# Sums of FFN weights made by accumulating DMAs in place of VectorE and GpSimd operations

## The chip, the cores and the metric

The kernel runs on one core of a Trainium2 chip (trn2). The metric is the device time of one execution in microseconds (us). Of the kernel before there are three timed runs and one profiled execution. Engine names are those of the profile: PE (TensorE), DVE (VectorE), ACT (ScalarE), POOL (GpSimd) and SP (the engine that only issues DMAs). PEld is PE's loading of weights.

## What is computed

One step of a two-layer streaming encoder for 1024 prompt frames and 64 frames of a running stream, 1088 columns in all, model width 1024, in fp32. Layer 0 is an SSD mixer (a gated state-space scan), layer 1 a chunk-band attention. Each is followed by a SwiGLU feed-forward layer (FFN) with a hidden width of 2816; the change touches only this part and what is done ahead of it:

```python
def swiglu(u, w_in, w_out):
    g, up = jnp.split(u @ w_in, 2, axis=-1)
    return (jax.nn.silu(g) * up) @ w_out
...
        xp = xp + rmsnorm(swiglu(rmsnorm(xp, nw[2]), ffn_w_in[layer], ffn_w_out[layer]), nw[3])
        xs = xs + rmsnorm(swiglu(rmsnorm(xs, nw[2]), ffn_w_in[layer], ffn_w_out[layer]), nw[3])
```

## The kernel before

**Products.** Every fp32 operand is split into a high part, rounded to the fp32r type that PE reads, and a low part, the rest. A product is three matmuls: high by high, high by low, low by high (L1338, L1339, L1340 in the FFN's first half). The high part of a weight tile is a cast on ACT, the low part a subtraction (method part, L354 and L355), on DVE unless another engine is named; or ACT writes the negated high part and an accumulating DMA from POOL adds the weights from DRAM to it (L350).

**Stages.** The head (weights, norms) lasts to about 97 us, the SSD scan with the input projection to 655, the output projection to 906, FFN-1 (u @ w_in, silu, product) of layer 0 from 918 to 1331, FFN-2 (@ w_out) to about 1575, the attention to about 2113 with its projection behind it, FFN-1 of layer 1 from 2260 to 2672 and FFN-2 to the end at 2918.

**FFN-1.** There are 22 pairs of weight tiles, gate and up. The columns are two halves, b = 0 with 512 and b = 1 with 576, each made of two quarters. A pair with its two quarters and two halves of the inner dimension is a 2 by 2 block product, which run_pair makes with seven products instead of eight (PRODS, in Strassen's manner). Six of the pairs are first run plainly for b = 0 (plain_pairs); then 16 pairs run for both halves, the first of them all seven products of b = 0 and then those of b = 1 ("apart"), the others alternately; at the end the six pairs of the start run for b = 1 alone. In this text the first pair, the middle and the tail of FFN-1 are these three parts. A product is 12 matmuls, of 256 columns for b = 0 and 288 for b = 1.

**Weights of a pair** (method pair). SP loads two raw tiles of 512 KB: r0 holds the blocks b11 and b21, r1 holds b12 and b22. POOL makes two differences into ta and tb (L302: b22 - b12, L303: b12 - b11), DVE completes them with two sums (L320, L321). Then r0, ta and tb are each split (L354, L355 on DVE), and b22 is split with its low half on POOL (L355, engine POOL; for two pairs per layer by the accumulating DMA L350). Rings of buffers: raw (2, and lent ones called rx), hl for split tiles (3), half for b22 (2), tt for ta and tb (2).

**Evacuation.** The seven products leave PSUM by adds on DVE (L1353, L1355, L1359, L1362, L1363, L1365, L1370) and activations on ACT (L1356, L1366). Two products per pair are made on POOL: u (L1367) and c (L1371). put_hid stores them to DRAM, and sum_one (L1469) and sum_two (L1477) make on DVE the sums of hidden tiles that FFN-2's seven products need; these wait for u and c.

**Weight sums for FFN-2.** FFN-2 is also a seven-product block, and four of its seven weight operands are sums of blocks of w_out. They are made during FFN-1: load_sums loads blocks (SP), sum_weights makes four DVE operations per job (L1414; 40 jobs, called from hook behind certain products), and SP stores the result to a DRAM tensor wsum, from which FFN-2 loads its tiles.

**What sets the order.** The order on PE is written by hand (the Stream st, with a planner clock st.t that advances by the cost of the matmuls). The other engines take their instructions in an order that a scheduler makes ahead of time, by priorities and its own estimates; each engine and each DMA queue then works strictly in that order. W.behind, W.loaded and the function behind fix places by dependences that cost no wait at run time.

**The scan.** It handles groups of output tiles of the input projection; in each group DVE evacuates the matmuls (L762), multiplies the decay matrices MT that SP has loaded (L886 the load, L895 the operation), POOL makes xe (L918), from which PE makes sp (L926), and y products (L963) that SP stores (yscr, L964).

## Time and profile before

| what | us |
|---|---|
| median of the timed runs | 2917.82 |
| lowest and highest of three | 2912.8, 2917.83 |
| profiled execution | 2919.82 |
| its span | 2918.0 |
| PE busy in it | 2852.8 |
| DVE, ACT, POOL busy | 2191.3, 1383.5, 726.5 |

Times inside the profile count from the start of its span. A row of a timeline gives the start, the duration, the engine, the line of the kernel, the operation, its output and inputs by name and shape, and in brackets how long the engine had been idle before it and which instruction's end released it. The granted clock is PE's, 1.00 at full speed. Busy times of matmuls overlap, so PE's rate is better read from the number of matmuls in a stretch.

### The profile page before, as it was taken

Reading aid. Unit: us, or ns where it says so; the run is one execution under the profiler, and the core shown is the slowest. Engines: PE = TensorE matmul, PEld = TensorE weight load, DVE = VectorE, ACT = ScalarE, POOL = GpSimd, SP = SyncE. Lnnn points to the kernel's source line nnn. Section 1 sums busy time; section 2 is a strip of 40 time slices with the busy share of each in tenths; the row PEclk is TensorE's granted clock in tenths of the full one; section 3 lists DMA queues with packets and bytes.
Section 4 is the critical chain, followed back from the end, with each engine's and each line's share of the span. In section 5 each row is a group of like instructions: output and inputs, shape, how many; then the busy total and the mean of one; then the engine's idle time right before and its main releaser. Section 6 shows DMA issues by size and latency. Waiting matters only on the chain. (4 is left out here: it accounts for less than half of the span.)

```text
span 2918.0 us, 58367 instructions
## 1 busy us (share of the span) xinstructions
PE 2852.8 (98%) x22094; PEld 2805.7 (96%) x22094; DVE 2191.3 (75%) x4994; ACT 1383.5 (47%) x2564; POOL 726.5 (25%) x900
## 2 busy tenths in 40 slices
PE   8999999999999999999998999999999999999999
PEld 8999999999999999999997899999999999999998
DVE  7987888885768667785569778777778876776567
ACT  6654546454444222244445556556565322334443
POOL 1333333331122343441021000000041334343011
PEclk9999999999999999999999999999999999999999
DMA  4423333244565556446564222222377455555656
GB/s 139 126 99 101 107 101 103 96 125 144 177 183 157 168 175 194 160 159 209 183 194 156 61 80 79 74 64 82 96 220 214 152 180 175 178 176 169 203 189 196
DMA packets 271530, 426.23 MB, mean 146 GB/s; under 512 B 25360, under 2 KB 202736, under 8 KB 271248
## 3 DMA queue, kind: packets, MB, share of 16 engines
q1 hardware_dynamic: 268016, 411.94, 44.4%
q0 software_dynamic: 3232, 10.56, 2.0%
q8 instruction: 174, 2.85, 0.4%
q14 instruction: 108, 0.88, 0.1%
HBM read 313.74 MB, written 104.19 MB: 143 GB/s over the span
## 5 line engine op out<-in xcount | busy, mean ns | idle before, releaser
L480 PE MATMUL mm<-r,hl 128*128 128x384 f32 (+2 forms) x1704 | 569.0, 334 | 6.1 <-DVE vt L1872 3.9
L481 PE MATMUL mm<-r,hl 128*128 128x384 f32 (+2 forms) x1704 | 551.4, 324 | 2.4 <-DVE r L1586 2.4
L482 PE MATMUL mm<-r,hl 128*128 128x384 f32 (+2 forms) x1704 | 551.1, 323 | 2.1 <-DMA hl<-in_w_in_dram 1.4
L1339 PE MATMUL px<-r,hl 128*128 128x288 f32 (+1 forms) x1184 | 348.1, 294 | 0.0
L480 PEld LDWEIGHTS mm<-r,hl 128*128 128x128 f32 x1704 | 323.4, 190 | 8.4 <-DVE vt L1872 4.2
L481 PEld LDWEIGHTS mm<-r,hl 128*128 128x128 f32 x1704 | 323.2, 190 | 3.3 <-DVE r L1586 3.0
L482 PEld LDWEIGHTS mm<-r,hl 128*128 128x128 f32 x1704 | 322.0, 189 | 2.8 <-DMA hl<-in_w_in_dram 1.7
L1340 PE MATMUL px<-r,hl 128*128 128x288 f32 x1056 | 312.7, 296 | 3.2 <-DVE hl L355 3.1
L1338 PE MATMUL px<-r,hl 128*128 128x288 f32 x1056 | 311.3, 295 | 2.8 <-DVE u L1353 2.1
L355 DVE TENSOR_TENSOR hl<-raw,hl 128x1024 fp32r<-128x1024 f32 (+2 forms) x172 | 193.7, 1127 | 99.1 <-ACT hl L354 98.8
L1712 PE MATMUL po<-r,hl 128*128 128x288 f32 (+1 forms) x856 | 246.9, 288 | 0.1
L1710 PE MATMUL po<-r,hl 128*128 128x288 f32 (+1 forms) x856 | 246.9, 288 | 0.0
L1711 PE MATMUL po<-r,hl 128*128 128x288 f32 (+1 forms) x856 | 246.9, 288 | 0.0
L1339 PEld LDWEIGHTS px<-r,hl 128*128 128x128 f32 x1184 | 223.0, 188 | 0.0
L354 ACT CAST hl<-raw 128x1024 fp32r<-128x1024 f32 (+2 forms) x172 | 166.5, 968 | 114.0 <-PE po L1712 34.3
L1340 PE MATMUL px<-rx,hl 128*128 128x256 f32 x768 | 215.0, 280 | 3.7 <-DVE hl L355 3.6
L1338 PE MATMUL px<-rx,hl 128*128 128x256 f32 x768 | 214.5, 279 | 1.5 <-ACT hl L354 1.5
L1340 PEld LDWEIGHTS px<-r,hl 128*128 128x128 f32 x1056 | 199.4, 189 | 4.6 <-DVE hl L355 4.6
L1338 PEld LDWEIGHTS px<-r,hl 128*128 128x128 f32 x1056 | 199.5, 189 | 3.7 <-DVE u L1353 2.5
L1339 PE MATMUL px<-rx,hl 128*128 128x256 f32 x640 | 178.9, 280 | 0.0
L1710 PEld LDWEIGHTS po<-r,hl 128*128 128x128 f32 x856 | 161.5, 189 | 0.0
L1712 PEld LDWEIGHTS po<-r,hl 128*128 128x128 f32 x856 | 160.9, 188 | 0.3 <-DVE hl L355 0.3
(385 smaller groups left out, 8152.2 us busy)
## 6 DMA issues: line engine op xcount, KB each, us to landing
raw<-in_w_f_dram SPq DMA_DIRECT2D x104, 512.0 KB, 4.2
raw<-in_w_in_dram SPq DMA_DIRECT2D x40, 512.0 KB, 3.9
MT<-ascr SPq DMA_DIRECT2D x48, 384.0 KB, 4.4
r<-hscr SPq DMA_DIRECT2D x58, 288.0 KB, 4.2
raw<-in_w_so_dram SPq DMA_DIRECT2D x32, 512.0 KB, 3.8
r<-in_w_f_dram SPq DMA_DIRECT2D x48, 288.0 KB, 3.4
wsum<-r SPq DMA_DIRECT2D x24, 576.0 KB, 3.4
r<-hscr SPq DMA_DIRECT2D x40, 256.0 KB, 4.2
```

The source lines that it names most:

```text
L354: self.nc.scalar.copy(h, v)
L355: (eng or self.eng or self.nc.vector).tensor_tensor(lo, v, h, op=ALU.subtract)
L480: PE.matmul(ps[:, :n], h_, xh, start=(first and i == 0), stop=False)
L481: PE.matmul(ps[:, :n], h_, xl, start=False, stop=False)
L482: PE.matmul(ps[:, :n], l_, xh, start=False, stop=(last and i == nk - 1))
L1338: PE.matmul(ps, wh, ah[:, k, :], start=(k == 0), stop=False)
L1339: PE.matmul(ps, wh, al[:, k, :], start=False, stop=False)
L1340: PE.matmul(ps, wl, ah[:, k, :], start=False, stop=(k == 3))
L1710: PE.matmul(ps, wh, xh, start=(k0 > 0 and i == ks[0]), stop=False)
L1711: PE.matmul(ps, wh, xl, start=False, stop=False)
L1712: PE.matmul(ps, wl, xh, start=False, stop=(k0 == 0 and i == ks[-1]))
```

## The change

The signs of the seven-product scheme are turned, so that the sums of weight blocks are plain sums without a difference. In the place of tb and ta stand T (s1), with the halves b11 + b12 and b12 + b22, and S (s2), with the halves b11 + b12 + b22 and the sum of all four. They are made as follows.

- **Pairs of FFN-1.** SP loads two 512-wide blocks into T (L282). When the planner's clock is 5.0 us further (ACC_W), POOL issues an accumulating DMA of 512 KB into T (L288). DVE makes S from T and r0 in two sums (L330, L331). S (s2) and T (s1) are split as before. The second raw load is only b22, 256 KB. The low half of b22 is always made by ACT's negated copy (L358) and an accumulating DMA (L359). The POOL operations L302, L303 and L355 are gone.
- **Sums for FFN-2.** weight_sums makes wsum of both layers during the scan, in DRAM: for each of four blocks per layer, copies by SP (L608 with 1.44 MB, L610 twice with 0.72 MB) and accumulating DMAs by POOL (L609 with 1.44 MB, L611 and L612 with 0.72 MB). Three steps are issued in each group of the scan from the fifth on. load_sums, sum_weights and their buffers are gone.
- **Products.** P4 now comes before P5, and some evacuations subtract where they added; their number is the same, and PE's order is the same.

DVE has 4120 rows of instructions instead of 4240, ACT 2100 instead of 2045, POOL 822 instead of 839, SP 1211 instead of 1248. The core of the diff:

```diff
+ACC_W = 5.0
...
+            while self.tq and self.tt.free():
+                it = self.tq.pop(0)
+                it["T"] = self.tt.get()
+                self.loaded = self.nc.sync.dma_start(it["T"].rearrange("p (e k) -> p e k", e=2), it["two"][0])
...
+                self.aq.append((self.clock() + ACC_W, it))
+            while self.aq and self.aq[0][0] <= self.clock():
+                it = self.aq.pop(0)[1]
+                self.nc.gpsimd.dma_start(it["T"], it["two"][1], accum_op=ALU.add)
+                it["added"] = True
...
-            ta, tb = it["T"] = self.tt.get(), self.tt.get()
-            g = self.nc.gpsimd.tensor_tensor
-            g(ta[:, 512:], b22, b12, op=ALU.subtract)
-            g(tb[:, :512], b12, b11, op=ALU.subtract)
...
-            self.part(it, "b22", self.half, b22, self.nc.gpsimd, it["pacc"] and it["src"][1][:, 512:])
...
+            self.part(it, "b22", self.half, r1[:, :512], None, it["src"][1])
...
+            T, S = it["T"], self.t2.get()
...
-                v(ta[:, :512], ta[:, 512:], b11, op=ALU.add)
-                v(tb[:, 512:], b21, ta[:, :512], op=ALU.subtract)
+                v(S[:, :512], T[:, 512:], r0[:, :512], op=ALU.add)
+                v(S[:, 512:], S[:, :512], r0[:, 512:], op=ALU.add)
...
-        for key, src in (("ta", ta), ("tb", tb)):
+        for key, src, ring in (("s2", it["S"], self.t2), ("s1", it["T"], self.tt)):
...
-    (P1, "r0", 0, 0), (P6, "ta", 0, 1), (P2, "r0", 512, 2), (P7, "ta", 512, 5),
-    (P5, "tb", 0, 3), (P4, "tb", 512, 6), (P3, "b22", 0, 4),
+    (P1, "r0", 0, 0), (P6, "s2", 0, 1), (P2, "r0", 512, 2), (P7, "s1", 512, 5),
+    (P4, "s2", 512, 6), (P5, "s1", 0, 3), (P3, "b22", 0, 4),
...
+    def weight_sums(layer):
+
+        w2, z, n = w_f2[layer], wsm_[layer], HF * P
...
+        steps = []
+        for g in range(4):
+            a, b, to = w2[2 * g], w2[2 * g + 1], z[:, g]
+            steps.append((
+                lambda g=g, to=to: sp(nc.sync.dma_start(to[:, 2:4, :], w2[2 * g:2 * g + 2, :, :n].rearrange("e p k -> p e k"))),
+                lambda b=b, to=to: pool(G.dma_start(to[:, 2:4, :], b.rearrange("p (e k) -> p e k", e=2), accum_op=ALU.add, max_dma_last_dim=4 * n)),
+                lambda a=a, to=to: (sp(nc.sync.dma_start(to[:, 0, :], to[:, 3, :])), sp(nc.sync.dma_start(to[:, 1, :], a[:, n:]))),
+                lambda a=a, to=to: pool(G.dma_start(to[:, 0, :], a[:, :n], accum_op=ALU.add)),
+                lambda to=to: pool(G.dma_start(to[:, 1, :], to[:, 0, :], accum_op=ALU.add)),
+            ))
+        for f in range(5 + 3):
+            for g in range(4):
+                if 0 <= f - g < 5:
+                    yield steps[g][f - g]
...
-        for grp in order:
+        staged = chain_of(weight_sums(0), weight_sums(1))
+        for i, grp in enumerate(order):
+            for _ in range(3 if i > 3 else 0):
+                next(staged, lambda: None)()
...
-                if (p_, t_ % 2) in ((P2, 0), (P7, 0), (P7, 1)):
-                    w = next((w for w in workers[::-1 if (p_, t_ % 2) == (P7, 0) else 1] if "job" in w), None)
-                    if w:
-                        sum_weights(w, last)
```

Three places show what moves. The first is POOL in the tail of layer 0's FFN-1, two pairs and a part of a third, before (u and c are the hidden products, half and tt weight tiles):

```order
L1367 TENSOR_TENSOR u_15602<-u_15602,c_15624 128x288
L355 TENSOR_TENSOR half<-raw,half 128x512
L303 TENSOR_TENSOR tt<-raw,rx 128x512
L1371 TENSOR_TENSOR c_15624<-p_15551,u_15566 128x288
L302 TENSOR_TENSOR tt<-raw 128x512
L1367 TENSOR_TENSOR u_15739<-u_15739,c_15761 128x288
L355 TENSOR_TENSOR half<-raw,half 128x512
L303 TENSOR_TENSOR tt<-raw,rx 128x512
L1371 TENSOR_TENSOR c_15761<-p_15685,u_15700 128x288
```

The same two pairs on POOL now:

```order
L1407 TENSOR_TENSOR u_15510<-u_15510,c_15525 128x288
L359 DMA half<-in_w_f_dram 128x512
L1411 TENSOR_TENSOR c_15525<-p_15458,u_15473 128x288
L288 DMA tt<-in_w_f_dram 128x1024
L1407 TENSOR_TENSOR u_15648<-u_15648,c_15663 128x288
L359 DMA half<-in_w_f_dram 128x512
L1411 TENSOR_TENSOR c_15663<-p_15593,u_15608 128x288
```

Between u and c stood two tensor operations on weights, and now there is one DMA issue; the sum for T is issued behind c.

The second place is DVE ahead of the first pair of layer 0's FFN-1, before (raw and tt are weight tiles, hl<-raw is the low half of r0, r<-r is work on the activations):

```order
L320 TENSOR_TENSOR tt<-tt,raw 128x512
L1312 TENSOR_TENSOR x<-mmx,x 128x256
L321 TENSOR_TENSOR tt<-raw,tt 128x512
L355 TENSOR_TENSOR hl<-raw,hl 128x1024
L1197 TENSOR_TENSOR r<-r 128x1152 x4
L355 TENSOR_TENSOR hl<-tt,hl 128x1024
```

And now (t_11192 is S; L364 is the former L355, L1236 the former L1197):

```order
L330 TENSOR_TENSOR t_11192<-tt,raw 128x512
L1352 TENSOR_TENSOR x<-mmx,x 128x256
L331 TENSOR_TENSOR t_11192<-t_11192,raw 128x512
L1236 TENSOR_TENSOR r<-r 128x1152 x4
L364 TENSOR_TENSOR hl<-raw,hl 128x1024
L1236 TENSOR_TENSOR r<-r 128x1152
L364 TENSOR_TENSOR hl<-t_11192,hl 128x1024
```

The low half of r0 has moved from ahead of the four r<-r operations to behind them, and stands behind the sums that wait for T.

The third place is SP's queue in the scan, before, around the fifth group (raw are weights of the input projection, yscr stores y, MT and ea are loads of decay factors):

```order
L262 DMA raw<-in_w_in_dram 128x1024 x2
L964 DMA yscr<-y 128x384 x2
L262 DMA raw<-in_w_in_dram 128x1024
L964 DMA yscr<-y 128x320
L262 DMA raw<-in_w_in_dram 128x1024
L886 DMA MT<-ascr 128x2x384 x2
```

And now at the same place:

```order
L268 DMA raw<-in_w_in_dram 128x1024 x2
L608 DMA wsum_116<-in_w_f_dram 128x2x1408 x2
L1000 DMA yscr<-y 128x384 x2
L268 DMA raw<-in_w_in_dram 128x1024
L1000 DMA yscr<-y 128x320
L268 DMA raw<-in_w_in_dram 128x1024
L610 DMA wsum_116<-wsum_116 128x1408
L610 DMA wsum_116<-in_w_f_dram 128x1408
L608 DMA wsum_116<-in_w_f_dram 128x2x1408
L1000 DMA yscr<-y 128x384
L922 DMA MT<-ascr 128x2x384
```

Five copies for the weight sums have come between the loads and stores, three of them between the last weight load and the next MT.

More of the change, by code (lines that the diff above doesn't have):

```diff
@@ L1 @@
 from contextlib import ExitStack
+from itertools import chain as chain_of
 import concourse.bass as bass
@@ L234, with __init__ @@
 class Weights:
-    def __init__(self, nc, raw, hl, half, tt):
-        self.nc, self.raw, self.hl, self.half, self.tt = nc, raw, hl, half, tt
+    def __init__(self, nc, raw, hl, half, tt, t2):
+        self.nc, self.raw, self.hl, self.half, self.tt, self.t2 = nc, raw, hl, half, tt, t2
         self.tc, self.pri, self.nsc = None, 0, 0
@@ L255, in plan @@
             self.sq.append(it)
+            if "two" in it:
+                self.tq.append(it)
     def load(self):
@@ L272, in advance @@
             moved = False
+            while self.tq and self.tt.free():
+                it = self.tq.pop(0)
+                it["T"] = self.tt.get()
+                self.loaded = self.nc.sync.dma_start(it["T"].rearrange("p (e k) -> p e k", e=2), it["two"][0])
+                if self.behind is not None:
+                    self.tc.add_manual_dep(self.loaded.ins, self.behind.ins.name, ORDER, reason="place in the order")
+                self.aq.append((self.clock() + ACC_W, it))
[3 more added lines that the diff above has]
+                it["added"] = True
             while self.lq and any(r.free() for r in self.raws):
@@ L316, in pair @@
             return False
-        if "sums" not in it:
+        if "b22" not in it and self.half.free():
+            self.part(it, "b22", self.half, r1[:, :512], None, it["src"][1])
+            it["of"][1].put()
+            return True
+        if "S" not in it:
+            if "added" not in it or not self.t2.free():
+                return False
+            T, S = it["T"], self.t2.get()
+            it["S"] = S
             v = self.nc.vector.tensor_tensor
             with self.tc.high_priority(self.pri):
-                v(ta[:, :512], ta[:, 512:], b11, op=ALU.add)
-                v(tb[:, 512:], b21, ta[:, :512], op=ALU.subtract)
+                v(S[:, :512], T[:, 512:], r0[:, :512], op=ALU.add)
+                v(S[:, 512:], S[:, :512], r0[:, 512:], op=ALU.add)
             it["of"][0].put()
-            it["sums"] = True
             return True
-        for key, src in (("ta", ta), ("tb", tb)):
+        for key, src, ring in (("s2", it["S"], self.t2), ("s1", it["T"], self.tt)):
             if key not in it:
@@ L329, in pair @@
                 self.part(it, key, self.hl, src)
-                self.tt.put()
+                ring.put()
                 return True
@@ L580, in drop_u, with sp, pool @@
             UC.put(c)
+    last_g = [None]
+    def weight_sums(layer):
+        w2, z, n = w_f2[layer], wsm_[layer], HF * P
+        def sp(x):
+            tc.add_manual_dep(x.ins, W.loaded.ins.name, ORDER, reason="place in the order")
+        def pool(x):
+            tc.add_manual_dep(x.ins, last_g[0].ins.name, ORDER, reason="place in the order")
+        steps = []
[12 more added lines that the diff above has]
+                    yield steps[g][f - g]
     order = []
@@ L1395, in behind @@
                     tc.add_manual_dep(x.ins, last.ins.name, ORDER, reason="place in the order")
-            def load_sums(w):
-                n = w["n"]
-                if not jobs[n]:
-                    return
-                w["job"] = g, c = jobs[n].pop(0)
-                z = w["z"] = w["get"]()[:, :, :n]
-                for e in range(2):
-                    src = w_f2[layer][2 * g + e].rearrange("p (h k) -> p h k", h=2)
-                    behind(nc.sync.dma_start(z[:, 2 * e:2 * e + 2, :], src[:, :, c:c + n]), W.loaded)
-            def sum_weights(w, last):
-                (g, c), z = w.pop("job"), w["z"]
-                n = z.shape[2]
-                b11, b21, b12, b22 = (z[:, i, :] for i in range(4))
-                for to, x, y, op in ((b22, b22, b12, SUB), (b12, b12, b11, SUB), (b11, b22, b11, ADD), (b21, b21, b11, SUB)):
-                    behind(V.tensor_tensor(to, x, y, op=op), last)
-                nc.sync.dma_start(wsm[:, :, g, c:c + n], z)
             def hook(p_, t_, last):
@@ L1639, in back @@
                 W.behind = None
-                R.put(len(workers) - 1)
-                assert not any(jobs.values()) and not any("job" in w for w in workers) and len(summed) == 2 * HF
+                assert len(summed) == 2 * HF
             phase[0], W.lent.cap = 2, LENT
```

72 lines of the change are left out of this document (28 added, 44 removed).

## The prediction

> **What bounds the kernel now.** I read the page's engine table first, then the windows by stage, then inside FFN-1 the waits of PE and DVE and the timelines of the stretches where PE idles. First the page, then windows (span; busy PE, PEld, DVE, ACT, POOL with instructions; granted clock; DMA share; GB/s): two stretches of the scan, then the first pair, the middle and the tail of FFN-1, layer 0 and layer 1.
>
> ```profile
> PE 2852.8 (98%) x22094; PEld 2805.7 (96%) x22094; DVE 2191.3 (75%) x4994; ACT 1383.5 (47%) x2564; POOL 726.5 (25%) x900
> ```
> ```profile
> 200.00:300.00 100.00, 100.00 (x709) 98.28 (x708) 80.73 (x209) 52.03 (x83) 36.98 (x61) 1.00 0.33 101
> 500.00:600.00 100.00, 100.00 (x695) 98.47 (x693) 81.92 (x213) 54.02 (x86) 37.10 (x58) 1.00 0.30 96
> ...
> 917.80:938.00 20.20, 17.30 (x127) 16.70 (x126) 14.71 (x24) 7.27 (x11) 4.95 (x5) 0.92 0.32 90
> 938.00:1256.00 318.00, 318.00 (x2563) 318.00 (x2562) 223.10 (x435) 97.73 (x163) 125.61 (x105) 1.00 0.56 179
> 1256.00:1331.00 75.00, 69.48 (x510) 67.37 (x508) 60.12 (x91) 29.47 (x47) 37.74 (x28) 1.00 0.45 141
> 2260.00:2284.00 24.00, 21.09 (x167) 20.50 (x166) 23.35 (x30) 14.29 (x18) 5.95 (x5) 1.00 0.26 72
> 2597.00:2672.00 75.00, 71.06 (x513) 69.18 (x512) 58.66 (x87) 28.28 (x44) 36.77 (x27) 0.98 0.44 141
> ```
>
> PE bounds it: 2852.8 of 2918.0 us, and the change leaves every matmul where it was. So it can win only where PE stands still, and lose wherever it makes PE wait. In the middle PE is busy 318.00 of 318 us at 318/2563 = 124.1 ns per matmul, an even mix of 256 and 288 columns; by width that is 116.8 and 131.4 ns. The tails hold 288-wide matmuls only: 510 need 67.0 us and took 75, 513 need 67.4: losses of 8.0 and 7.6 us, **15.6 together**, part idle, part slow matmuls. The first pair runs 84 narrow matmuls and then wide ones: 84 x 0.1168 + 43 x 0.1314 = 15.5 of 20.20 us, and 20.7 of 24.00 us: losses of 4.7 and 3.3, **8.0 together**. Nothing else in FFN-1 can be won.
>
> What makes the tail late is in the waits of DVE there, and in the timelines of POOL and of DVE (start, us, instruction, idle time before it):
>
> ```profile
> DVE y L1469 <- POOL c L1371: 5.3, 3, 2.8
> DVE y L1477 <- POOL c L1371: 4.4, 2, 2.8
> ```
> ```profile
> 1297.89 1.24 POOL L1367 TENSOR_TENSOR u<-u,c 128x288 f32<-128x288 f32 x1 [1.65 <-ACT u L1366]
> 1299.09 1.75 POOL L355 TENSOR_TENSOR half<-raw,half 128x512 fp32r<-128x512 f32 x1
> 1300.80 1.28 POOL L303 TENSOR_TENSOR tt<-raw,rx 128x512 f32<-128x512 f32 x1
> 1302.04 0.80 POOL L1371 TENSOR_TENSOR c<-p,u 128x288 f32<-128x288 f32 x1
> 1309.22 1.30 POOL L302 TENSOR_TENSOR tt<-rx 128x512 f32<-128x512 f32 x1 [6.38 <-DVE hl L355]
> ```
> ```profile
> 1293.64 1.23 DVE L355 TENSOR_TENSOR hl<-tt,hl 128x1024 fp32r<-128x1024 f32 x1
> ...
> 1302.88 0.46 DVE L1469 TENSOR_TENSOR y<-u,c 128x288 f32<-128x288 f32 x1 [2.83 <-POOL c L1371]
> 1303.25 0.45 DVE L1355 TENSOR_TENSOR p<-px,p 128x288 f32<-128x288 f32 x1
> 1303.62 1.21 DVE L355 TENSOR_TENSOR hl<-rx,hl 128x1024 fp32r<-128x1024 f32 x1
> ...
> 1309.43 2.17 DVE L355 TENSOR_TENSOR hl<-tt,hl 128x1024 fp32r<-128x1024 f32 x1
> ...
> 1324.52 0.46 DVE L1469 TENSOR_TENSOR y<-u,c 128x288 f32<-128x288 f32 x1 [0.85 <-POOL c L1371]
> ```
>
> POOL works through two weight subtractions (1.75 and 1.28 us) before the hidden product c of L1371. DVE, in order, stands 2.83 us at L1469 for that c, and behind it wait the evacuation L1355 and the low half of the next weights, L355, which PE then waits for. When POOL has no weights left, the same wait is 0.85 us.
>
> **The change part by part.** *Tail.* POOL's L302, L303 and L355 go; in their place stand two DMA issues per pair. The waits for c were 9.7 us in five; five of 0.85 are 4.3, so DVE is given 5.4 us back in this tail. The low half also shortens from 2.17 towards 1.23 us where POOL was in a tensor operation (L302 ran from 1309.22). The Trainium skill, "SBUF — State Buffer", section "SBUF: two separate sides", says that a VectorE operation with two SBUF inputs and a GpSimd operation reading SBUF take a shared port pair by an exclusive lock; the two rows agree with that. Giving back 5.4 us of DVE time and some slow subtractions against 8.0 us of loss, I take three quarters: **-11.7 us** for both tails; bounds 0 and -15.6. What is late next is ACT's silu and POOL's own product, 0.85 us of wait each, and T.
>
> T, the sum that s1 is made of and S starts from, now comes by two DMAs. Their prices:
>
> ```profile
> hl<-in_w_f_dram POOLq DMA_DIRECT2D x11, 512.0 KB, 8.4
> raw<-in_w_f_dram SPq DMA_DIRECT2D x104, 512.0 KB, 4.2
> ...
> MT<-ascr SPq DMA_DIRECT2D x48, 384.0 KB, 4.4
> ```
>
> The plain load (4.2) hides in the planner's 5.0 us before the accumulate; 5.0 + 8.4 + two sums of about 0.7 + a split of 1.2 = 16.0 us. A tail pair is 84 x 0.1314 = 11.0 us, and T's ring has two buffers, so 22.1 us are there: 6 us of cover. In the middle a pair is 168 matmuls, 20.8 us, and the cover is wide: **0**. A gain is excluded there too, since PE idles nowhere.
>
> *Weight sums on DVE.* They are 160 operations:
>
> ```profile
> L1414 DVE TENSOR_TENSOR r<-r 128x288 f32<-128x288 f32 x96 | 50.5, 526 | 0.9 <-DMA r<-in_w_f_dram 0.5
> L1414 DVE TENSOR_TENSOR z<-z 128x272 f32<-128x272 f32 x64 | 28.9, 451 | 0.1
> ```
>
> 79.4 us of DVE go, nearly all beside the middle's full PE: worth **0**. Evacuations change sign, not number. ACT's 40 negated copies lie beside an ACT that is busy 97.73 of 318 us.
>
> *First pair.* Here are PE's stalls in layer 0, DVE's weight work, and the last POOL DMA ahead of it:
>
> ```profile
> 925.21 0.38 PE L1338 MATMUL px<-rx,hl 128*128 128x256 f32 x1 [1.49 <-ACT hl L354]
> ...
> 927.08 0.58 PE L1340 MATMUL px<-rx,hl 128*128 128x256 f32 x1 [1.37 <-DVE hl L355]
> ```
> ```profile
> 909.48 1.77 DVE L320 TENSOR_TENSOR tt<-tt,raw 128x512 f32<-128x512 f32 x1 [1.49 <-POOL tt L302]
> 911.17 0.41 DVE L1312 TENSOR_TENSOR x<-mmx,x 128x256 f32<-128x256 f32 x1
> 911.51 0.67 DVE L321 TENSOR_TENSOR tt<-raw,tt 128x512 f32<-128x512 f32 x1
> 912.11 1.21 DVE L355 TENSOR_TENSOR hl<-raw,hl 128x1024 fp32r<-128x1024 f32 x1
> 913.24 5.15 DVE L1197 TENSOR_TENSOR r<-r 128x1152 fp32r<-128x1152 f32 x4
> ```
> ```profile
> 904.38 0.84 POOL L350 DMA_DIRECT2D hl<-in_w_f_dram  x1 [5.16 <-PE mmx L482]
> ```
>
> By the orders shown above, the low half of r0 moves behind the two sums and four operations that took 5.15 us. If T's accumulate is issued at 905.2, right behind POOL's last one, it lands at 913.6; sums to 915.0, the four to 920.2, r0's half to 921.4. The pair starts at 917.8 and needs it about 0.3 us later: a stall of 3.3 us that was not there. Against it, T needs no second sum, so the two stalls on the last weights (1.49 + 1.37) can go. I take +1.5 for layer 0. In layer 1 DVE is busy 23.35 of 24.00 us, so every slowed sum that goes helps: I take -0.5. Together **+1.0**; bounds -8.0 (both losses gone) and +8 (both stalls added and the old ones kept, with the slow matmuls behind them).
>
> *Scan.* The copies and accumulates of the weight sums are 8 x 1.44 + 16 x 0.72 = 23.0 MB each (1.44 is 128 x 2 x 1408 fp32 numbers). Nothing in the trace copies DRAM to DRAM; the nearest rows are the two queues (packets, MB, share of the 16 engines' span) and what waits there (us in total, times, longest):
>
> ```profile
> q1 hardware_dynamic: 268016, 411.94, 44.4%
> q0 software_dynamic: 3232, 10.56, 2.0%
> ```
> ```profile
> DVE craw L762 <- PE mm L482: 18.0, 12, 3.0
> DVE MT L895 <- DMA MT<-ascr: 16.0, 12, 2.4
> ```
> ```profile
> 571.77 1.22 POOL L918 TENSOR_TENSOR xe<-xd,dec 128x384 f32<-128x384 f32 x1
> ```
> ```profile
> 574.75 0.83 PE L926 MATMUL sp<-xe,Bn 128*128 128x128 f32 x6
> ```
>
> 411.94 MB in 1296 us of engine time is 318 GB/s, 10.56 in 58 is 181. So the copies take 72 us of all 16 engines and the accumulates 127, spread over some 430 us: a DMA share of 0.33 becomes about 0.8. PE idles nowhere in 200-600, so no gain is possible. The cost: 24 issues of 0.84 us on POOL are under the 1.76 us between xe's end (572.99) and PE's need (574.75). Where an accumulate waits for another DMA, POOL stands up to 8.4 us, 6.6 more than that slack; the order has about four such places. So 0 to 26 us from POOL; DMA and SP delays are the rival below. I take **+2**, near the lower end, since the halo copies and y products that stand behind POOL's issue in most places already wait for other engines.
>
> Sum: -11.7 + 1.0 + 2.0 = **-8.7 us**. The profiled execution took 2919.8 us (span 2918.0), 2.0 above the median of 2917.8; so 2911.1 for it and **2909** for the median.
>
> **Rivals.** (1) *Nothing measurable.* The tail gives only 5.4 us, DVE's returned time of one tail spread over both, and the first pairs and the scan take 3: about 2915. For it: the 0.85 us waits stay, and tail DVE is 80% busy (60.12 of 75).
>
> (2) *Slower: the scan's queue.* MT loads stand on SP's queue behind 1.44 MB copies. DVE has waited for MT at landing 12 times, so those have no slack; about nine lie in the changed stretch. A copy ahead costs 1.44/318 = 4.5 us to 1.44/181 = 8.0; DVE is ahead of PE by up to 3.0 us (the wait for L482), so each costs PE 1.5 to 5.0, nine cost 14 to 45. At 25: 2917.8 - 11.7 + 1 + 25 = 2932. It decides when MT lands over 3 us later. Against it: y stores that wait for POOL stand between most copies and MT. The Trainium skill, "DMA: Bandwidth & Descriptors", section "Rules for kernel authors", says that spreading DMAs over issuing engines gains no bandwidth, as all run on the same 16 DMA engines; the trace gives one share for both queues and can't test it.
>
> (3) *Slower: T late in the tail.* If accumulates land in twice 8.4 us beside a busy DVE, 16.0 becomes 24.4 against 22.1 us: 2.3 per two pairs, 14 us over twelve, and the tail gain is lost: 2917.8 + 14 + 1 + 2 = 2935. The same page on SBUF warns that VectorE's two-port operations can keep GpSimd from writing DMA descriptors; here 8.4 against 4.2 us may hold some of that, or only the read before the write.
>
> (4) *All of it.* Both tails and both first pairs run clean and the scan costs nothing: up to -20, 2898.
>
> **How the numbers follow.** Forecast 0.52, rival (1) 0.20, (2) 0.18, (3) 0.05, (4) 0.05. About 0.2%, 5.8 us, can be told from no change. Of the forecast's 0.52, 0.40 lies beyond 5.8 us; with (4) and a little of (1) faster is 0.46; same 0.12 + 0.16 = 0.28; slower 0.26. The forecast's own range is 2903 to 2916. The whole range reaches from all of it (2898) to the scan's queue (2932).
>
> **What would show it.** Right: DVE's waits for c in the tails fall to about 0.85 each and the 75 us windows to about 69; the scan keeps PE at 100 of 100 with a DMA share near 0.8; the first pair's stall moves to r0. Wrong: PE idle in 230-655 behind DVE's MT or POOL's xe, or s1 and s2 halves that wait for T in the tail.

## The result and the profile after

The changed kernel takes 2943.84 us in the median of 4 runs (2942.78 to 2953.46), the kernel before 2917.82 in runs beside it (2912.8 to 2922.23): a ratio of 1.0097, 95% interval 1.007 to 1.0124. The forecast was 2909 with a range of 2898 to 2932; it was slower by 26.0 us where 9 us less had been forecast. The profiled execution took 2944.86 us, with a span of 2943.2.

First the page's engine table and DMA queues of the changed kernel:

```profile
PE 2858.4 (97%) x22094; PEld 2810.2 (95%) x22094; DVE 2131.8 (72%) x4834; ACT 1424.9 (48%) x2616; POOL 605.3 (21%) x880
...
q1 hardware_dynamic: 241584, 400.40, 42.0%
q0 software_dynamic: 19808, 67.19, 13.3%
```

DVE and POOL have less to do, as meant (2191.3 and 726.5 us before), and the POOL queue q0 moves 67 MB where it moved 10.6. PE has the same 22094 matmuls in the same order as before. So the start of the n-th matmul in both traces says where time was lost. The table gives the delay that each stage adds (end of the stage less its start), in us:

| stage (us of before) | delay added |
|---|---|
| scan (200 to 655) | +28.5 |
| out-projection (655 to 906) | -0.4 |
| first pair, layer 0 (906 to 938) | +3.2 |
| middle, layer 0 (938 to 1256) | 0.0 |
| tail, layer 0 (1256 to 1331) | -3.6 |
| FFN-2, attention (1331 to 2230) | -4.1 |
| first pair, layer 1 (2230 to 2400) | +4.9 |
| middle, layer 1 (2400 to 2597) | 0.0 |
| tail, layer 1 (2597 to 2672) | -3.3 |

The -4.1 isn't a gain of the change: kernels below that change nothing there show between -4.1 and +1.4 against this one execution of before, which was about 2 us above its own median. So a long stage that a kernel leaves alone can differ by 5 us between executions, and one where PE never waits by a few tenths. The first pairs and the tails can be read more closely: seven kernels below have the same FFN-1 as the changed one, and with it they show +1.9 to +3.7 and +3.8 to +6.5 in the first pairs of layer 0 and 1, and -4.0 to -2.0 and -3.6 to -2.8 in the tails.

Here are stretches of the scan, then the middle and the two tails of FFN-1 (columns as in the prediction):

```profile
400.00:500.00 100.00, 90.25 (x643) 86.44 (x642) 70.38 (x198) 48.49 (x71) 38.94 (x61) 0.97 0.75 206
500.00:600.00 100.00, 100.00 (x691) 98.54 (x690) 84.22 (x216) 52.98 (x83) 40.38 (x67) 1.00 0.72 204
```
```profile
974.00:1287.60 313.60, 313.60 (x2530) 313.60 (x2529) 192.64 (x347) 104.08 (x172) 75.14 (x89) 1.00 0.59 157
1287.60:1359.00 71.40, 69.16 (x510) 68.69 (x509) 58.05 (x96) 34.54 (x56) 19.63 (x22) 0.98 0.80 217
...
2625.80:2697.50 71.70, 69.36 (x512) 68.99 (x511) 58.27 (x97) 34.46 (x56) 19.65 (x22) 0.98 0.83 219
```

The scan's DMA share is 0.7 to 0.8, as forecast, but PE no longer stays at 100 of 100. The middle is untouched, and each tail has come down from 75 to about 71.5 us.

Where the scan waits is in the waits of DVE and PE from 107 to 684 us (the scan's length now):

```profile
DVE MT L931 <- DMA MT<-ascr: 43.2, 18, 9.5
...
PE mm L489 <- DVE zs L798: 12.4, 8, 7.0
...
PE mm L489 <- DVE craw L798: 7.3, 6, 2.6
```

DVE's waits for MT at landing went from 16.0 us, 2.4 at most, to 43.2 and 9.5, and PE, which had next to no wait for evacuations in the scan before, has 14 of them now, 19.7 us in all. The longest of them shows how, on POOL, SP, DVE and PE in turn:

```profile
444.44 1.17 POOL L609 DMA_DIRECT2D wsum<-in_w_f_dram  x1
```
```profile
444.75 1.85 SPq L922 DMA_DIRECT2D MT<-ascr  x2
```
```profile
458.93 1.20 DVE L931 TENSOR_SCALAR MT<-MT,nac 128x128 f32<-128x128 f32 x6 [9.53 <-DMA MT<-ascr]
460.05 0.55 DVE L798 TENSOR_TENSOR zs<-mm,rb 128x384 f32<-128x384 f32 x1
```
```profile
460.65 0.64 PE L489 MATMUL mm<-r,hl 128*128 128x320 f32 x1 [7.01 <-DVE zs L798]
```

An accumulate of 1.44 MB is issued just before two MT loads. MT lands 14 us after its issue, where the median before was 4.4; DVE, in order, stands 9.53 us at L931 with the evacuation L798 behind it; PE waits 7.01 us for that. Behind this stall the matmuls first start 0.27 us apart, where ahead of it they started 0.145 apart. How the rest of the 28.5 us, beyond the 19.7 of waits, divides up was not worked out. POOL itself stood 19.8 us for landings of wsum in the scan, yet PE's waits for POOL's xe come to 0.6 us. The queues and landings of this stretch (443 to 460) agree:

```profile
q0 software_dynamic: 412, 2.16, 68.0%
q1 hardware_dynamic: 1077, 1.50, 27.3%
...
MT<-ascr SPq DMA_DIRECT2D x2, 384.0 KB, 14.6
```

POOL's queue had 68% of all 16 engines' time and SP's 27. The Trainium skill, "DMA: Bandwidth & Descriptors", section "Queues, rings and completion order", says that each DMA engine takes turns between its queues a packet at a time. The trace agrees so far: both queues moved bytes in this stretch, and MT took 14.6 us where its median was 4.4 before. It can't show the turns themselves.

### The profile page after: what moved, and what is told of

Its sections match the earlier page's. It is cut to its first block, busy times and chain, and to the rows that moved or that the text cites. A ratio compares the mean times of both kernels' runs of the same rounds, so it can differ in the third digit from the quotient of the medians.

```text
span 2943.2 us, 58213 instructions
## 1 busy us (share of the span) xinstructions
PE 2858.4 (97%) x22094; PEld 2810.2 (95%) x22094; DVE 2131.8 (72%) x4834; ACT 1424.9 (48%) x2616; POOL 605.3 (21%) x880
## 3 DMA queue, kind: packets, MB, share of 16 engines
q8 instruction: 173, 2.83, 0.4%
## 5 line engine op out<-in xcount | busy, mean ns | idle before, releaser
L364 DVE TENSOR_TENSOR hl<-raw,hl 128x1024 fp32r<-128x1024 f32 (+2 forms) x171 | 195.1, 1141 | 92.9 <-ACT hl L363 92.3
```

The lines of the kernel that those rows point to most:

```text
L364: (eng or self.eng or self.nc.vector).tensor_tensor(lo, v, h, op=ALU.subtract)
```

## The experiments

Each kernel is the changed one with the edit shown, unless the text says otherwise. Lines in the diffs are those of the file that is edited. Losses of a stage are worked out as in the table above, each from one profiled execution; the scan is 200 to 655.

**Which DMAs of the scan cost.** Four kernels on one chip.

No sums at all:

```diff
-        staged = chain_of(weight_sums(0), weight_sums(1))
+        staged = iter(())
-                        src = wsm_[layer][:, g, y, k0 * P:(k0 + nk) * P]
+                        src = w2[2 * g + y % 2][:, (y // 2 * HF + k0) * P:(y // 2 * HF + k0 + nk) * P]
```

> The changed kernel without any DMA for the FFN-2 weight sums: FFN-2 reads plain blocks of w_out of the same sizes in place of the sums, so its numbers are others. Theory BYTES (the copies and accumulates fill the 16 DMA engines, MT comes late, DVE stands at it): the scan's 28.4 us vanish, 2915.5. Theory FIFO (copies ahead of MT on SP's queue) and theory POOL (POOL stands waiting for landings): the same, 2915.5. Theory ORDER (the scheduler's other order of DVE costs, whatever the DMAs do) would also give 2915.5 here. If the scan still loses over 5 us, the loss isn't from the weight sums at all (turned signs, ACT table loads).

Measured: 2916.89 us against 2916.75, ratio 1.0005 (0.9995 to 1.0015); scan -0.8. So the scan's loss comes from the DMAs alone, and the rest of the change is worth nothing together: first pairs +2.7 and +6.5, tails -4.0 and -2.8.

Only the copies, the POOL steps replaced by nothing:

```diff
-                lambda b=b, to=to: pool(G.dma_start(to[:, 2:4, :], b.rearrange("p (e k) -> p e k", e=2), accum_op=ALU.add, max_dma_last_dim=4 * n)),
+                lambda b=b, to=to: None,
```

(and the same for L611 and L612.)

> Only the copies on SP (23 MB), the accumulates on POOL left out, so the sums lack their second summand. BYTES: the loss goes with the DMA time, 72 of 199 us of it copies: about 10 us left in the scan, 2926. FIFO: all of it stays, about 2943. POOL: all of it goes, 2916. ORDER: between, not told.

Measured: 2923.54, ratio 1.0025 (1.0014 to 1.0036); scan +6.4.

Only POOL's DMAs, as plain copies, and no copies on SP:

```diff
-                lambda a=a, to=to: pool(G.dma_start(to[:, 0, :], a[:, :n], accum_op=ALU.add)),
+                lambda a=a, to=to: pool(G.dma_start(to[:, 0, :], a[:, :n])),
```

(the same for the others, L608 and L610 replaced by nothing, FFN-2 as in the first kernel.)

> Only the 24 DMAs on POOL, as plain copies of the same bytes instead of accumulates, without SP's copies that they waited for; FFN-2 reads plain blocks. BYTES: at the rate of plain transfers 72 us of DMA time, about 10 us of the 28 left, 2926; if what POOL issues crowds the other queue more than SP's own copies do, up to 2934. FIFO: nothing is left, 2916. POOL: most of it goes, since only L612 behind L611 waits for a landing, about 2918.

Measured: 2925.47, ratio 1.0031 (1.0019 to 1.0043); scan +7.4.

All of them, small:

```diff
-                lambda a=a, to=to: pool(G.dma_start(to[:, 0, :], a[:, :n], accum_op=ALU.add)),
+                lambda a=a, to=to: pool(G.dma_start(to[:, 0, :128], a[:, :128], accum_op=ALU.add)),
```

> All copies and accumulates stay in number, place and dependence, but each moves 128 columns in place of 1408 (a eleventh of the bytes, 2.1 MB each way); FFN-2 reads plain blocks. BYTES and FIFO: a eleventh of the loss, about 2918. POOL (waits for landings, which keep their fixed part): about a third stays, 2925. ORDER: nearly all stays, about 2940.

Measured: 2923.09, ratio 1.0023 (1.0012 to 1.0033); scan +3.5 in the profiled execution, which took 2.5 us less than the median. DVE's waits for MT in the run with copies and in that with POOL's plain DMAs (200 to 660 us):

```profile
DVE MT L931 <- DMA MT<-ascr: 18.4, 11, 4.3
```
```profile
DVE MT L931 <- DMA MT<-ascr: 20.1, 8, 4.9
```

What follows: the order of instructions, the issues and the waits for landings with few bytes are worth 3.5 of 28.5 by the profiled executions. By the medians, against the kernel without sums, the small DMAs cost 6.2 us, the copies 6.7 and POOL's plain DMAs 8.6; so how much of each half is due to its bytes stays open, and what is clear is that neither half, nor what is left with few bytes, comes near 28.5. FIFO falls, since POOL's DMAs alone, with nothing added to SP's queue, cost as much as the copies there. Each half alone gives 6 to 7 us in the scan, and the whole, with accumulates in place of POOL's copies, four times that. The Trainium skill, "DMA: Bandwidth & Descriptors", section "Rules for kernel authors", says that spreading DMAs over issuing engines doesn't help, since all run on the same 16 DMA engines; the POOL-only run agrees with that, as DVE waits 20.1 us for MT there and 18.4 in the run with SP's copies.

**Is it the accumulating, and is it MT?** Two more kernels. The accumulates as plain copies, with all copies and all waits kept:

```diff
-                lambda to=to: pool(G.dma_start(to[:, 1, :], to[:, 0, :], accum_op=ALU.add)),
+                lambda to=to: pool(G.dma_start(to[:, 1, :], to[:, 0, :])),
```

(the same for L609 and L611.)

> The changed kernel with the 24 accumulating DMAs on POOL turned into plain copies of the same bytes, at the same places and with the same waits; the sums then lack a summand. The runs with only the copies and with only plain POOL copies lost 6.4 and 7.4 us in the scan, the whole 28.5. Theory ACCUMULATE (the accumulate's slow packets hold the 16 DMA engines: 181 GB/s against 318): the scan loses about 14, 2930 in all. Theory LOAD (two such streams together are too much, whatever their kind): it stays over 23, 2940.

Measured: 2929.94, ratio 1.0046 (1.0033 to 1.0059); scan +13.0, near the sum of the two halves. ACCUMULATE holds. POOL's queue in the scan (200 to 660 us), of the changed kernel and of this one, and DVE's wait for MT in this one (200 to 680):

```profile
q0 software_dynamic: 4480, 23.07, 27.2%
```
```profile
q0 software_dynamic: 4480, 23.07, 14.8%
```
```profile
DVE MT L931 <- DMA MT<-ascr: 23.9, 12, 5.0
```

The same packets and bytes hold the 16 engines for 27.2% of 460 us = 125 us as accumulates and for 68 us as copies. So 15.5 of the 28.5 us come from accumulating in place of copying (13 by the medians of the two kernels). That they come by way of the longer hold agrees with MT's waits, 40.4 us in the changed kernel (200 to 660) and 23.9 here, but nothing else was varied to show it.

MT not loaded:

```diff
-            nc.sync.dma_start(MT, bass.AP(ac_.tensor, row, [[0, P], [NCH * P, 2], [1, 384]]))
...
-                    last = V.tensor_scalar(m_, m_, nac[:, c, 2 * j + e:2 * j + e + 1], 0.0, op0=ALU.subtract, op1=ALU.max)
+                    last = V.tensor_scalar(m_, pcs[:, :CHL[c]], nac[:, c, 2 * j + e:2 * j + e + 1], 0.0, op0=ALU.subtract, op1=ALU.max)
```

> The changed kernel without the loads of MT: DVE's operation reads a constant tile of the same size in their place, so the decay factors are others; all weight sums stay. Theory MT (late MT at DVE is what costs): the scan's loss falls from 28 to under 8, 2922. Theory CROWD (every load is late, and POOL stands for landings): it stays over 15, 2931 or more; some fall is due anyway, since 16 MB of loads are gone.

Measured: 2925.91, ratio 1.0029 (1.0019 to 1.0038). The scan loses 5.1 with all copies and accumulates in place; q0 still holds 27.3% there. What PE still waits for at the evacuation of z is one stall:

```profile
PE mm L489 <- DVE zs L798: 2.8, 1, 2.8
```

MT is the victim. Some of the fall is due to the loads that are gone, 32 of 384 KB in this stretch; how much wasn't told apart. It isn't the share of the DMA engines alone: that was 0.63 here (200 to 660) with a loss of 5.1, and 0.60 in the kernel without accumulating, which lost 13.0.

**Mending the scan.** DVE's work on MT put later, with a second edit in FFN-1, where the low halves of the last two plain weight tiles are made by DVE:

```diff
+            yield 0, MT_W
             m3 = MT[:, :, :n]
...
-            yield 0, SSD_D, lambda: (g, s) in cb_done and so["A"] == q and so["C"] >= q - 2 and st.t >= so["tA"]
+            yield 0, SSD_D - MT_W, lambda: (g, s) in cb_done and so["A"] == q and so["C"] >= q - 2 and st.t >= so["tA"]
...
-        W.plan(*[dict(src=[w1[i]], acc=t_ < NACC or t_ == NB0 - 1) for t_ in range(NB0) for i in (ORD[t_], FT + ORD[t_])])
+        W.plan(*[dict(src=[w1[i]], acc=t_ < NACC) for t_ in range(NB0) for i in (ORD[t_], FT + ORD[t_])])
```

(MT_W = 4.0.)

> The changed kernel with two edits far apart. In the scan, DVE's operations on MT (and what follows them) are put 4 us of the planner's clock later behind the MT load, so that DVE's queue reaches them later. Theory MT (the loss is DVE standing at L931 for a late MT, with PSUM evacuations queued behind): DVE's waits for MT fall from 40 us to under 15, the scan's loss from 28 to under 12. Theory CROWD (all loads late, raw and ea too; MT is only where it shows): the waits move to other lines, the loss stays over 20. In FFN-1, the low halves of the last two plain weight tiles are made by DVE instead of an accumulating DMA that stands behind T's on POOL: if that queue place is the cause, PE's 6.1 us stall ahead of layer 0's first pair goes, and the first pair's loss falls from +3.2 to about -2 (layer 1: from +4.5 to about 0); if T itself is the cause, the stall only moves to r0's low half and 2 to 3 us are won. Total: 2943.8 - 18 - 9 = about 2917 by MT and queue place, about 2938 by the others.

Measured: 2948.27, ratio 1.0105 (1.0088 to 1.0123). The scan still loses 25.4; the waits in it (200 to 680):

```profile
DVE MT L933 <- DMA MT<-ascr: 25.8, 10, 11.4
...
PE mm L490 <- DVE zs L799: 14.0, 5, 9.3
```

The waits for MT fell only from 40 to 26 us, with a longest of 11.4: four microseconds are too few for landings that come 10 late. So this run, which should have spoken for MT, did not; the one without MT loads decides. First pair of layer 0: +0.2 instead of +3.2; layer 1: +12.0 instead of +4.9 (more of that below).

The transfers in pieces (m is 352 columns):

```diff
+        def paced():
+            for f in chain_of(weight_sums(0), weight_sums(1)):
+                f()
+                yield 0, 2.5
...
-                    yield steps[g][f - g]
+                    for c in range(0, n, m):
+                        yield lambda s=steps[g][f - g], c=c: s(c)
```

> All copies and accumulates in four pieces each, one piece every 2.5 us of the planner's clock from the fifth group on, the same bytes and the same share of the DMA engines on average. Theory BURST (a 1.44 MB transfer in flight makes MT wait behind up to 11 us of packets): landing of MT stays under 8 us, the loss falls from 28 to 12 or less, 2928. Theory LOAD (the share near 0.75 is the cause): the loss stays over 22, about 2940; the added 120 issues on POOL may make it worse.

Measured: 2963.69, ratio 1.0157 (1.0137 to 1.0178). To 600 us of before the scan lost 16.0 instead of 28.1, with MT's longest wait at 5.9; then 24.5 more in its last 55 us. There POOL stood for landings, one piece after another, with xe queued behind (a row of POOL, and PE's wait):

```profile
655.60 0.81 POOL L614 DMA_DIRECT2D wsum<-wsum  x1 [6.44 <-DMA wsum<-in_w_f_dram]
```
```profile
PE sp L965 <- POOL xe L957: 13.8, 2, 13.5
```

Pieces make MT's longest wait shorter, and by chance of place they bring in the other cost, POOL in order. BURST is neither shown nor excluded by this run.

**Sums elsewhere, and the first pair.** All sums on DVE in the middle, with one buffer, since the changed kernel's S leaves no room for the two of before; nothing in the scan, and the last plain tiles on DVE:

```diff
+                if p_ in (P2, P3) and len(ops[1].hl) == len(OPI) and (jobs or workers) and t_ >= NB0 and not phase[0]:
...
+                    for w in workers:
+                        if "job" in w:
+                            sum_weights(w, last)
+                        if jobs:
+                            load_sums(w)
```

> The changed pairs of FFN-1, but the FFN-2 weight sums made on DVE again in the middle of FFN-1 (as plain sums, 80 operations per layer, one buffer), nothing added to the scan, and the low halves of the last two plain weight tiles on DVE. If the middle's full PE hides 79 us of DVE work, the middle stays at 0 against before, and the total is that of the kernel without sums less the first pairs' gain: 2917 - 7 = 2910. If one buffer and DVE's queue make the weights of the pairs late, the middle loses 5 or more.

Measured: 2998.85, ratio 1.0273 (1.0255 to 1.0291). The middle of layer 0 loses 38 us, and layer 1 loses 36 from 2284 to 2597. DVE's wait in the middle of layer 0 (940 to 1290):

```profile
DVE r L1453 <- DMA r<-in_w_f_dram: 59.5, 12, 9.3
```

The 79 us of DVE work were free before because their loads came far ahead: DVE's waits for them in layer 0's FFN-1 were 0.3 us then. The work itself has cover; a wait in DVE's order has none.

Layer 1's sums by DMAs in the attention:

```diff
+    def staged_sums():
+        for f in weight_sums(1):
+            f()
+            yield 0, 22.0
+
+    st.spawn(staged_sums(), 30.0)
```

> As the run with DVE sums, but the sums of layer 1 are made by copies and accumulating DMAs in DRAM during the attention, one step each 22 us of the planner's clock (the DMA share there was 0.2 to 0.3). If what costs in the scan is late loads that DVE or PE stand at, it costs nothing where loads have room: attention within 1 us of the run with DVE sums, 2910. If accumulating DMAs on POOL cost by themselves (POOL standing for landings in order), the attention loses 5 to 10.

Measured: 2967.15, ratio 1.017 (1.0155 to 1.0186); 36 of it from layer 0's middle as before. The attention from 1700 on is unchanged (within 1 us); from 1585 to 1700 it loses 5.6 (3.8 in the next run), where the first steps lie. The middle of layer 1, now without sums, is back to 0.0. So the expectation was missed on the total. For the attention it held but for the start, whose loss is in the range given for accumulates that cost by themselves; PE's waits there are on DVE and ACT, and none is on POOL or a DMA, so what causes it stays open.

As that, with S not raised in priority for the first pair:

```diff
-            with self.tc.high_priority(self.pri):
+            with self.tc.high_priority(0 if self.pri == HIP else self.pri):
                 v(S[:, :512], T[:, 512:], r0[:, :512], op=ALU.add)
```

> As the run before it, but without the raised priority for the first pair's sums S, so that DVE makes r0's low half ahead of them and doesn't stand for T there. If T's landing is what holds the first pair, 2 to 3 us per layer more are won, 2905; if not, the same as the run before it, 2910, or a us or two worse, since S is later.

Measured: 2956.93, ratio 1.0141 (1.012 to 1.0163). The first pair of layer 1 goes from +12.2 to +6.2, that of layer 0 stays near -1 (-1.3 and -0.6). So the place of S in DVE's order matters in layer 1 and not in layer 0; the rows are shown further down, where the first pairs are explained.

The spread version:

```diff
-        staged = chain_of(weight_sums(0), weight_sums(1))
+        staged = weight_sums(0)
         for i, grp in enumerate(order):
-            for _ in range(3 if i > 3 else 0):
+            for _ in range(2 if 14 > i > 3 else 0):
```

(with the attention steps of above from 140 us on, S as above, and the last plain tiles on DVE in layer 0 only.)

> A version that takes the runs so far together: layer 0's sums alone in the scan, two steps in each of ten groups; layer 1's in the attention, one step each 18 us, from 140 us behind its start; the last plain weight tiles split by DVE in layer 0 only; S without raised priority for the first pair. By the stages: scan +8 (half the bytes), first pairs -1 and about 0, tails -7, attention -3: 2915, the same as before. If the loss in the scan comes from each 1.44 MB accumulate singly, it is +14, and the whole 2921; if it grows faster than the bytes, +4, and 2911.

Measured: 2933.24, ratio 1.0057 (1.0036 to 1.0078), from 2924.11 to 2941.78, a wide spread. The scan lost 9.9 with half the bytes, against 28.5 with all. But the profiled execution is the fastest of the six, 9 us under their median, so whether the loss grows faster than the bytes isn't shown. Layer 1's first pair lost 11.6, which had been put at 0. Two waits of PE stand there: 3.4 us for the accumulate of the last plain tile, which was left on POOL in this layer, and 5.9 us for ACT's cast of S.

T of each first pair on POOL by two operations, the next accumulate held behind them, 15 chunks of layer 0's sums on DVE, one a pair:

```diff
+        if it["eng"] and "added" not in it:
+            if "T" not in it:
+                return False
+            T, g = it["T"], self.nc.gpsimd.tensor_tensor
+            g(T[:, 512:], r1[:, :512], r1[:, 512:], op=ALU.add)
+            self.first = g(T[:, :512], r0[:, :512], r1[:, :512], op=ALU.add)
```

> The changed pairs of FFN-1, but in each layer's first pair T is made by two operations on POOL from the raw tiles, and the second pair's accumulate is held behind them in POOL's order. Layer 0's sums for FFN-2: 15 of 20 chunks on DVE in the middle, one per pair, loaded most of a pair ahead; a quarter by DMAs in the scan, one step in every second group; layer 1's by DMAs in the attention. Theory T (the first pair waits for T's two DMAs and for the accumulate queued behind them): both first pairs are as before within 1 us. Theory DVE (layer 1's first pair is bound by DVE's 23 of 24 us): layer 1 still loses 3 or more. By stages: scan +2, first pairs 0, middle 0, tails -7, attention -3: 2910, below the kernel before. If the middle loses again as in the run with all sums on one buffer, DVE's in-order waits for loads are to blame, 2925.

Measured: 2926.12, ratio 1.003 (1.002 to 1.004). Scan +5.5 with an eighth of the DMAs, first pairs +1.7 and +4.0, middles 0.0, tails +1.8 and -3.5. The profiled execution is again the fastest, 7.6 us under the median, so these are low figures. With loads a pair ahead the middle hides the sums again. T by DMA is no longer in it, and layer 1's first pair still loses 4.0: there PE waits 4.6 us for ACT's cast of S, and ACT stood for a raw load ahead of that cast:

```profile
2262.33 0.62 ACT L371 CAST half<-raw 128x512 fp32r<-128x512 f32 x1 [10.43 <-DMA raw<-in_w_f_dram]
...
2263.78 1.03 ACT L377 CAST hl<-t 128x1024 fp32r<-128x1024 f32 x1
```

The loss is of the size that theory DVE gave, but this wait, of an engine in order for a load, is in neither theory.

**One part alone, on the kernel before.** The low half of b22 by DMA in all pairs:

```diff
-            W.plan(dict(src=[w1[ORD[t_]], w1[FT + ORD[t_]]], pacc=t_ in (NB0, NB0 + 1)))
+            W.plan(dict(src=[w1[ORD[t_]], w1[FT + ORD[t_]]], pacc=True))
```

> The kernel before with one part of the change alone: the low half of b22 is made by ACT's negated copy and an accumulating DMA in all pairs, not in two per layer. Theory POOL PLACE (the tail is late because u and c stand behind weight subtractions on POOL): one of the two subtractions between u and c goes, DVE's waits for c fall from 9.7 to about 5, the tails give back about half of what the whole change gave there, -3.5 in all: 2914. Theory DVE LOAD (the tail is late because DVE is busy with slow sums): nothing is won, 2917.5. If the added DMAs or ACT copies cost in the middle or at the first pair: 2920 or more.

Measured: 2911.59 in 12 runs against 2916.93 in 27 beside them, ratio 0.9984 (0.9974 to 0.9995): the only version here that is faster than the kernel before. The tail of layer 1 gives -4.3, that of layer 0 +0.2. POOL and then DVE in the tail of layer 0:

```profile
1297.78 1.74 POOL L303 TENSOR_TENSOR tt<-raw,rx 128x512 f32<-128x512 f32 x1
1299.49 0.80 POOL L1371 TENSOR_TENSOR c<-p,u 128x288 f32<-128x288 f32 x1
1300.24 0.86 POOL L350 DMA_DIRECT2D half<-in_w_f_dram  x1
```
```profile
1300.33 0.46 DVE L1469 TENSOR_TENSOR y<-u,c 128x288 f32<-128x288 f32 x1 [1.59 <-POOL c L1371]
...
1307.11 0.76 DVE L1506 TENSOR_TENSOR r<-r 128x576 fp32r<-128x576 f32 x1 [4.46 <-ACT r L1505]
```

The DMA has gone behind c, and DVE's wait for c falls from 2.83 to 1.59 us. Over the whole tail these waits fall from 9.7 to 3.8 us in layer 0 and from 9.3 to 4.7 in layer 1, as POOL PLACE said. In layer 0 another wait takes its place: DVE stands 4.46 us at L1506, the split of a hidden tile for FFN-2, for ACT's cast of it.

In the tail's pairs alone:

```diff
-            W.plan(dict(src=[w1[ORD[t_]], w1[FT + ORD[t_]]], pacc=t_ in (NB0, NB0 + 1)))
+            W.plan(dict(src=[w1[ORD[t_]], w1[FT + ORD[t_]]], pacc=t_ < NB0 + 2))
```

> The same in the tail's six pairs only (besides the two of before). POOL PLACE: as the run before it, 2914, if the middle hides the DMAs; better than it by what they cost otherwise.

Measured: 2916.1 in 11 runs, ratio 0.9999 (0.999 to 1.0007); tails 0.0 and -4.9. Its profiled execution shows the same tails as the run before it, and its median shows no gain. So the gain of 0.16% stands for the first of the two by its interval, which ends close to 1; that the tail of layer 1 is its source isn't shown, since here the same gain of the tail brings the median nothing.

## Why the prediction was wrong, step by step

**The scan's term (+2 us) is the step that failed.** It measured +28.5. The working put the cost of the accumulates on POOL (issues, and waits for landings, 0 to 26 us), took a value near the lower end because POOL's neighbours wait anyway, and left what the DMAs do to other loads to a rival with 0.18. POOL's part came out near what was assumed: PE waited 0.6 us for xe. The transfers were sized rightly: DMA time 127 us for accumulates (125 measured) and a share of about 0.8 (0.69 to 0.80 in the four stretches of 100 us from 200 on). What was not drawn from these numbers is that DVE takes MT at landing with no slack, at 12 places in the profile of before, so that a longer landing goes straight to DVE, and what exceeds DVE's lead over PE (its longest wait for PE there was 3.0 us) goes on to PE. That is also the sign of being wrong that the prediction had named, PE idle behind DVE's MT. The rival had this chain, its decision point (MT over 3 us later) and a price of 25 us; its share in the chances was too low. Its cause was half right: it blamed copies ahead of MT in SP's queue. Copies alone cost 6.4, POOL's stream alone as plain copies 7.4, both 13.0, and accumulating in place of copying 15.5 more. So its price came near the measured loss by luck, since it was worked out for the copies, which cost a quarter of it.

**The first pairs (+1.0; bounds -8 and +8)** measured +3.2 and +4.9, together 8.1, at the upper bound. The step that failed is the place of T's accumulate on POOL: the working issues it right behind POOL's last one, and in layer 0 foresaw a stall on r0 from there. In the changed kernel it stands ahead of that last one. POOL, DVE and PE there:

```profile
937.51 0.88 POOL L288 DMA_DIRECT2D tt<-in_w_f_dram  x1 [9.93 <-DMA tt<-in_w_f_dram]
938.10 1.20 POOL L359 DMA_DIRECT2D hl<-in_w_f_dram  x1
```
```profile
943.06 0.69 DVE L330 TENSOR_TENSOR t<-tt,raw 128x512 f32<-128x512 f32 x1 [6.88 <-DMA tt<-in_w_f_dram]
```
```profile
947.26 0.58 PE L491 MATMUL mmx<-rx,hl 128*128 128x256 f32 x1 [6.13 <-DMA hl<-in_w_f_dram]
```

POOL stood 9.93 us for T's plain load, and behind it in POOL's order stood the accumulate of the last plain weight tile, L359, for which PE waited 6.13 us, before the first pair had begun. DVE's wait for T (6.88 us) was foreseen; a stall of PE on r0 did not come. The delay rose by 8.5 us at this stall, and 5.3 came back within the pair, where the two old stalls (1.49 and 1.37) are gone. In layer 1 the changed kernel has the same stall (2250 to 2315):

```profile
PE mmx L491 <- DMA hl<-in_w_f_dram: 4.0, 1, 4.0
```

With that tile on DVE the loss of layer 0 is gone (+0.2, -0.2, -1.3, -0.6 and 0.0 in the five versions that have it). In layer 1 that remedy loses 12 us, and the rows show why. DVE and PE in the run with layer 1's sums in the attention, then PE in the run after it, with S not raised:

```profile
2290.39 0.69 DVE L330 TENSOR_TENSOR t<-tt,raw 128x512 f32<-128x512 f32 x1 [3.98 <-DMA tt<-in_w_f_dram]
...
2303.35 3.88 DVE L1236 TENSOR_TENSOR r<-r 128x1152 fp32r<-128x1152 f32 x3
2307.16 1.22 DVE L364 TENSOR_TENSOR hl<-raw,hl 128x1024 fp32r<-128x1024 f32 x1
```
```profile
2308.42 0.58 PE L1380 MATMUL px<-rx,hl 128*128 128x256 f32 x1 [13.10 <-DVE hl L364]
```
```profile
2299.93 0.58 PE L1378 MATMUL px<-rx,hl 128*128 128x256 f32 x1 [7.45 <-ACT hl L363]
```

With S raised, DVE stands 3.98 us for T and then makes S, its low half, other weight tiles and splits of activations (L1236) without a pause, and r0's low half comes last: PE waits 13.10 us for it. With S not raised, r0's low half is in time and S is late, behind those splits: PE waits 7.45 us for its cast. DVE's order in a stretch with little idle time is what costs in both, and T's landing is 4 us of the first.

**The tails (-11.7)** gave -3.6 and -3.3, between the bounds. The mechanism was right: the waits of DVE for c, 9.7 us in layer 0's tail before, are gone there, and in layer 1 the 9.3 us of before are 0.6. What the sum lacked is a new stall at the start of each tail. DVE's wait in layer 1, then PE's one stall in layer 0 and DVE ahead of it:

```profile
DVE y L1475 <- POOL c L1411: 0.6, 1, 0.6
```
```profile
1295.24 0.40 PE L1380 MATMUL px<-r,hl 128*128 128x288 f32 x1 [2.15 <-DVE hl L364]
```
```profile
1291.12 2.93 DVE L1512 TENSOR_TENSOR rx<-rx 128x512 fp32r<-128x512 f32 x4
1293.97 1.22 DVE L364 TENSOR_TENSOR hl<-tt,hl 128x1024 fp32r<-128x1024 f32 x1
```

DVE splits hidden tiles (L1512) first, and the low half of T (L364) for the tail's first pair stands behind them: PE idles 2.15 us. The same stall in layer 1 is 2.3 us. Against the kernel before, the delay rises by 3.7 us at this stall in layer 0 and falls by 7.3 in the rest of the tail; in layer 1 it rises by 3.3 and falls by 6.6. So behind their starts the tails gave back 13.9 us, more than the 11.7 forecast, and the stalls took 7.0 of them. In layer 0's tail of 71.4 us, 71.4 - 67.0 - 2.1 = 2.3 us more than the matmuls need go in slow matmuls (granted clock 0.98). The rival in which T comes late did not happen: DVE's waits for T sum to 4.9 us in layer 0's tail and 7.2 in layer 1's, and no wait of PE there is for T's landing.

**The middle (0)** was right in both layers to 0.1 us: DVE's busy time in layer 0's 318 us (969.6 to 1287.6 now) fell from 223 to 195 us and PE's didn't change. The run without sums says the same of the 79 us of DVE work as a whole.

**The sum.** Had the scan cost 2, the time would have been 26.5 us less, about 2917, no change, and the kernel without sums measured just that, 2916.89. The forecast's gain needed the tails at three quarters and the first pairs at +1.0, and both came out at the poor side. The rival with late MT loads had its price; its chance should have been weighed by the 12 places where MT has no slack. One sum of the prediction doesn't agree with its own terms: both tails and both first pairs are 15.6 + 8.0 = 23.6 us, not 20, so the lower end of the range stood 3.6 us too high; this had no bearing on the outcome.

## What to carry to other kernels

Before moving bytes into a stage because its DMA engines are a third busy, look for loads that an in-order engine takes at landing: what they are late by goes straight to what is queued behind them. An operation that only follows in a full stage costs nothing, and one that waits there for its load costs the whole wait. When DMAs are moved to another engine's queue, list what already stands in that queue with a wait of its own: an accumulate that waits for its load holds back every later one.

## What was not expected of the hardware

Accumulating DMAs from DRAM into DRAM held the 16 DMA engines 1.84 times as long as plain copies of the same 23.07 MB and 4480 packets (27.2% against 14.8% of 460 us). Two streams that cost the scan 6.4 and 7.4 us alone cost 13.0 together and 28.5 when one accumulates: the two plain streams nearly add up, and the jump comes with accumulating. MT's median landing in the scan rose only from 4.4 to 5.6 us while its worst over the whole run went from 5.8 to 15.0, so the median of landings did not show the loss.
